# Split-precision matmuls in which the products with the low part of the weights come last

## The chip, the cores and the metric

One core of one Trainium2 chip runs the whole program in one launch. The metric is device time in microseconds (us). The core's engines are called by short names: PE is TensorE (PEld its weight loads), DVE is VectorE, ACT is ScalarE, POOL is GpSimd, SP is SyncE, which issues the transfers of the weights. SBUF is the core's working memory, PSUM the small memory into which PE accumulates.

## The reference

256 tokens of width 1024 in float32 go through two blocks. The first has a mixer of two attention kinds and then a feed-forward layer (PEER) that picks 128 of 16384 experts for each token. The second has two layers, each a mixer, a convolutional gated feed-forward and a gated input. Around each part stands a root-mean-square norm. Cut to what matters here:

```python
def peer_ffn(xn, w_query, subkeys, u_tab, v_tab):
    q = (xt @ w_query).reshape(T, 8, 2, 128)
    s = einsum('thpd,hpkd->thpk', q, subkeys)          # scores of 2 x 128 sub-keys
    ...                                                # top 16 per half, top 16 of 256 sums
    act = gelu(einsum('thkd,td->thk', u_tab[expert], xc))
    w = gate * act
    return einsum('thk,thkd->td', w, v_tab[expert])

def second_block(...):
    for i in range(2):
        hn = rmsnorm(h, mix_norm[i])
        h = h + (mixer_ab(hn, ...) if i == 0 else mixer_c(hn, ...))
        h = h + conv_glu_ffn(rmsnorm(h, ffn_norm[i]), ...)
        gate = sigmoid(rmsnorm(h, ple_norm[i]) @ ple_gate[i])
        h = h + gate * (p[i] @ ple_proj[i])
```

## The kernel before

**Split products.** PE multiplies in a rounded 32-bit type. To keep float32 accuracy, each operand is split in two: a high part, which is the value rounded, and a low part, the rest. A product is then three matmuls into one PSUM bank: high by high, high by low, low by high. Activations are split once per norm into xTh and xTl (L301 to L303: ACT copies the high part, DVE subtracts). Weights are split as they stream in: `wstart` (L104) has SP load tiles of 128 x 1024 into the ring `raw`, `wsplit` (L111) has ACT copy the high part `hi` (L114) and then DVE or POOL subtract to get `lo` (L117). Which of the two takes a tile is set by a repeating pattern: "V" is DVE and "G" is POOL. Most stages have "V"; the stage with the top-k has "G", and the stage with the routing products, below, has "VG", which gives every other tile to POOL. The rings hold 3 raw, 4 hi and 4 lo tiles, and a few more where memory is free.

**The three loops that use them.** `xs` (L182) makes outputs with tokens on partitions: each half tile of weights takes 6 matmuls of 512 columns for each of the two token tiles. `ws` (L255) makes outputs with features on partitions: each half tile takes 24 matmuls of 256 columns, three for each of 8 slices k. `peer_v` (L933) sums over the experts' second table into four PSUM banks that stay open for the whole stage; each expert group takes 12 matmuls of 512 columns. In `peer_v` the first operand is split as well, into wh and wl, once for each group.

**Stages.** The program is a chain: first norm, mixer, query, top-k (beside `peer_u` for experts of the first half), routing products, `peer_v`, then the second block with `mixer_ab`, feed-forward, gate, block C, feed-forward and gate. At each seam, the last `xs` of a stage holds back some tiles so that the norm (`norm_tile`, L324) of token tile 0 is made while tile 1 is still multiplied. The norm is a sum of squares on ACT, nx on DVE (L339), a power on POOL (L340), xn on DVE (L346, three pieces), transposes on PE (`tsplit`, L359, matmuls at L362), and the split of the result. In this stretch DVE also makes `lo` for the next stage's first tiles. "The query" and "block C's keys" are the first `xs` calls behind two of these norms.

**The stage with the routing products.** Here two things run merged: `peer_u` (L876) for the experts of the second half, which is a `ws` and keeps PE busy, and `peer_g` (L898), which builds the gate of each token and expert. `peer_g` goes through 32 blocks of eight tokens, numbered from 0 here. In a block DVE makes two tiles E (L911, comparisons of the picked indices with an iota), then, twice, for four tokens each: ACT copies the one E to a float32 operand h (L916), DVE multiplies the other by the gate into another h (L917), PE makes four products of them in PSUM (`sm`, L921), and the result is multiplied on DVE into the table act (L927, act0 for the first half of the experts, act1 for as many of the second half as are already made) or copied by ACT where the activation isn't made yet (L929). `peer_u` applies the gelu on ACT (L886, L889) and multiplies by what is there (L887). So in each block DVE and ACT each have a dozen instructions from `peer_g`, `peer_u` and `wsplit`, whose shares change from block to block: act1 grows on DVE and shrinks on ACT.

**What sets the order.** Engines run their own queues in order. The order in each queue isn't written by hand: a scheduler, which has the program order, a cost for each instruction and the dependencies, places instructions on each engine; only a few are pinned to program order. So the order on DVE, ACT and POOL follows from when the scheduler finds operands to be ready and wanted, also where the code of these engines isn't touched.

## Time and profile before

| | us |
|---|---|
| median of 3 runs | 1646.69 |
| lowest, highest | 1646.3, 1653.85 |
| the profiled execution, its own time | 1641.96 |
| its span on the core | 1640.2 |
| PE busy | 1607.5 (98%) |
| DVE busy | 1206.6 (74%) |
| ACT busy | 943.2 (58%) |
| POOL busy | 290.2 (18%) |
| `lo` on DVE (L117) | 506.0, 413 instructions |
| `lo` on POOL (L117) | 249.2, 96 instructions |
| `hi` on ACT (L114) | 537.8, 509 instructions |

The profile is of one execution; its clock is the full one (0.999 granted). The busy shares are means over all stages. A matmul's busy time is counted with its modelled end, and matmuls overlap: rows that follow each other at a start-to-start distance of 0.11 us (256 columns) show a duration of 0.28 us. So lengths of PE's work are read from starts, not from durations. The same holds, by less, for DVE, whose instructions begin about 0.08 us before the one before has ended.

### The profile page before, as it was taken

To read this page: it belongs to the slowest core of one execution; us is meant where nothing else is said; L and a number is where in the kernel's file an instruction comes from. 1 tells how busy PE (TensorE), PEld (TensorE's weight loads), DVE (VectorE), ACT (ScalarE), POOL (GpSimd) and SP (SyncE) were. 2 spreads that over 40 slices of the span, in tenths; PEclk is the share of its full clock that TensorE was granted. 3 is DMA by queue.
4 is the path that set the end of the run, shared out by engine and by line. 5 is a ranking of instruction groups with operands and counts; after the bars stand their busy time and mean duration, and the time that the engine had idled before them with its cause. 6 is when DMAs were issued, how large, how long until landed. Compare 5 with 4: busy or idle time off the path is not lost.

```text
span 1640.2 us, 27505 instructions
## 1 busy us (share of the span) xinstructions
PE 1607.5 (98%) x10596; PEld 1435.0 (87%) x10596; DVE 1206.6 (74%) x2172; ACT 943.2 (58%) x1435; POOL 290.2 (18%) x145
## 2 busy tenths in 40 slices
PE   7999999999999999999999999989999999999998
PEld 5878999999999997888888879869998777899986
DVE  7766597908999996666555567878896686699845
ACT  5555545446666665555555557457664456576633
POOL 2000499993333220000000001100000000000000
PEclk9999999999999999999999999999999999999999
DMA  7536556554444446656666555437666662376661
GB/s 248 178 123 214 157 169 195 167 178 132 147 135 143 141 151 209 192 192 226 218 192 190 192 178 176 124 98 228 190 195 191 191 227 85 98 227 194 194 192 63
DMA packets 83200, 284.54 MB, mean 173 GB/s; under 512 B 10556, under 2 KB 14589, under 8 KB 82942
## 3 DMA queue, kind: packets, MB, share of 16 engines
q1 hardware_dynamic: 82924, 282.72, 54.8%
q8 instruction: 83, 1.36, 0.3%
q14 instruction: 47, 0.39, 0.1%
q10 hardware_dynamic: 146, 0.07, 0.0%
HBM read 280.64 MB, written 2.12 MB: 172 GB/s over the span
## 4 chain that ended last, share of the span: by engine, by line
PE 80%; DVE 15%; ACT 2%; issue 1%; DMA 1%; POOL 1%; SPq 0%; DVEq 0%; ACTq 0%; POOLq 0%
PE mm L957 21%; PE mm L268 11%; PE mm L269 11%; PE mm L270 11%; PE mm L214 6%; PE mm L213 6%; PE mm L212 6%; DVE h L917 5%; DVE lo L117 3%; DVE E L911 2%; DVE act L927 1%; PE sm L921 1%; PE sm L605 1%; PE sm L362 1%; PE sm L577 1%
## 5 line engine op out<-in xcount | busy, mean ns | idle before, releaser
L114 ACT ACTIVATE hi<-raw 128x1024 fp32r<-128x1024 f32 x509 | 537.8, 1059 | 329.7 <-PE mm L269 143.4
L117 DVE TENSOR_TENSOR lo<-raw,hi 128x1024 fp32r<-128x1024 f32 x413 | 506.0, 1230 | 172.9 <-ACT hi L114 169.8
L268 PE MATMUL mm<-xTh,hi 128*128 128x256 f32 x1992 | 559.1, 281 | 0.2
L269 PE MATMUL mm<-xTl,hi 128*128 128x256 f32 x1992 | 552.7, 278 | 0.0
L270 PE MATMUL mm<-xTh,lo 128*128 128x256 f32 x1992 | 552.4, 277 | 0.0
L268 PEld LDWEIGHTS mm<-xTh,hi 128*128 128x128 f32 x1992 | 374.5, 188 | 1.5 <-ACT xTh L302 0.7
L270 PEld LDWEIGHTS mm<-xTh,lo 128*128 128x128 f32 x1992 | 375.1, 188 | 0.0
L269 PEld LDWEIGHTS mm<-xTl,hi 128*128 128x128 f32 x1992 | 374.5, 188 | 0.6 <-DVE xTl L303 0.3
L117 POOL TENSOR_TENSOR lo<-raw,hi 128x1024 fp32r<-128x1024 f32 x96 | 249.2, 2615 | 204.8 <-ACT hi L114 194.5
L340 POOL TENSOR_TENSOR ny<-nx,expo 128x1 f32<-128x1 f32 x14 | 13.0, 925 | 928.2 <-DVE nx L339 928.2
L917 DVE TENSOR_TENSOR h<-E,gate 128x512 f32<-128x512 bf16 x64 | 116.0, 1815 | 1.8 <-PE sm L921 1.8
L213 PE MATMUL mm<-lo,xTh 128*128 128x512 f32 x256 | 102.3, 400 | 5.9 <-DVE lo L117 3.6
L212 PE MATMUL mm<-hi,xTh 128*128 128x512 f32 x256 | 103.6, 405 | 3.0 <-ACT xTh L302 2.8
L214 PE MATMUL mm<-hi,xTl 128*128 128x512 f32 x256 | 101.5, 398 | 0.5 <-DVE xTl L303 0.3
L916 ACT ACTIVATE h<-E 128x512 f32<-128x512 bf16 x64 | 72.3, 1133 | 43.3 <-DVE E L911 39.9
L1379 DVE SCALAR_TENSOR_TENSOR fc<-mm,cw,fc 128x255 f32<-128x255 f32 (+1 forms) x176 | 84.3, 479 | 3.1
L957 PE MATMUL mm<-hi,xTh 128*128 128x512 f32 x256 | 80.1, 394 | 1.4 <-DVE act L887 1.0
L911 DVE TENSOR_TENSOR E<-sel,iota 128x1024 bf16<-128x1024 bf16 x64 | 48.5, 795 | 43.7 <-POOL iota L905 38.1
L957 PE MATMUL mm<-hi,wh 128*128 128x512 f32 x256 | 79.9, 393 | 0.0
L957 PE MATMUL mm<-hi,xTl 128*128 128x512 f32 x256 | 79.6, 391 | 0.0
L957 PE MATMUL mm<-hi,wl 128*128 128x512 f32 x256 | 79.3, 391 | 0.0
L957 PE MATMUL mm<-lo,xTh 128*128 128x512 f32 x256 | 79.3, 390 | 0.0
(304 smaller groups left out, 2359.6 us busy)
## 6 DMA issues: line engine op xcount, KB each, us to landing
raw<-in_peer_uT SPq DMA_DIRECT2D x128, 512.0 KB, 3.9
raw<-in_peer_v SPq DMA_DIRECT2D x128, 512.0 KB, 4.3
raw<-in_ffn_up_ws SPq DMA_DIRECT2D x88, 512.0 KB, 4.7
raw<-in_ffn_down_a SPq DMA_DIRECT2D x40, 512.0 KB, 4.5
raw<-in_w_in_xs SPq DMA_DIRECT2D x20, 512.0 KB, 4.7
raw<-in_ab_ws SPq DMA_DIRECT2D x16, 512.0 KB, 4.6
raw<-in_ple_gate_xs SPq DMA_DIRECT2D x16, 512.0 KB, 4.2
raw<-in_w_query_ws SPq DMA_DIRECT2D x12, 512.0 KB, 4.9
```

The lines of the kernel that those rows point to most:

```text
L114: nc.scalar.activation(hi, raw, AF.Copy)
L117: x = eng.tensor_tensor(lo, raw, f32(hi), op=ALU.subtract)
L212: nc.tensor.matmul(p, xh[:, k, t], hi[:, w], start=n == 1 and kk == 0, stop=False)
L213: nc.tensor.matmul(p, xh[:, k, t], lo[:, w], start=False, stop=False)
L214: nc.tensor.matmul(p, xl[:, k, t], hi[:, w], start=False, stop=n == total[c] and kk == 1)
L268: nc.tensor.matmul(o, hi[:, w], xh[:, k, :], start=k == 0, stop=False)
L269: nc.tensor.matmul(o, hi[:, w], xl[:, k, :], start=False, stop=False)
L270: nc.tensor.matmul(o, lo[:, w], xh[:, k, :], start=False, stop=k == 7)
L911: v.tensor_tensor(E[q], x[:, :, None, :].to_broadcast([P, T1, P, T2]), iota[:, None].to_broadcast([P, T1, P, T2]), op=ALU.is_equal)
L917: v.tensor_tensor(B.rearrange("p t j -> p j t"), E[1][:, i], gate[:, None, t0:t0 + T2].to_broadcast([P, P, T2]), op=ALU.mult)
L957: nc.tensor.matmul(self.acc[tt][c], st_[:, t], mv[:, c * 512:c * 512 + 512], start=first and j == js[0] and i == 0, stop=j == last and i == 2)
L1379: v.scalar_tensor_tensor(c[:, o + sft:o + S], p[:, o:o + S - sft], cw[:, wi, j:j + 1], c[:, o + sft:o + S], op0=ALU.mult, op1=ALU.add)
```

## The change

In each of the three loops the matmuls that use the low part of the weights are put behind those that use the high part. In `xs`, for a half tile and a token tile, the order was high-high, high-low(weights), low-high for the first slice and again for the second; it becomes high-high for both, low-high for both, and then the two with `lo`. In `ws`, for a half tile, the three matmuls of each of 8 slices become 16 with `hi`, and behind them 8 with `lo`. In `peer_v`, where the weights are the moving operand, the 8 matmuls with `hi` for both token tiles come first and then the 4 with `lo`. The number of matmuls, their shapes, the flags that open and close a sum and the other engines' code stay. The sums are the same in another order. Lines below the edits are shifted by at most one in the new file.

```diff
--- before.py
+++ after.py
@@ -205,13 +205,12 @@
                 acc[tt, c] = self.mm_ps()
             p = acc[tt, c]
             n = seen[tt, c] = seen.get((tt, c), 0) + 1
-            for kk in range(2):
-                k = kp * 2 + kk
-                w = slice(kk * 512, kk * 512 + 512)
-                t = slice(tt * P, tt * P + P)
-                nc.tensor.matmul(p, xh[:, k, t], hi[:, w], start=n == 1 and kk == 0, stop=False)
-                nc.tensor.matmul(p, xh[:, k, t], lo[:, w], start=False, stop=False)
-                nc.tensor.matmul(p, xl[:, k, t], hi[:, w], start=False, stop=n == total[c] and kk == 1)
+            t = slice(tt * P, tt * P + P)
+            for x, y in ((xh, hi), (xl, hi), (xh, lo)):
+                for kk in range(2):
+                    nc.tensor.matmul(p, x[:, kp * 2 + kk, t], y[:, kk * 512:kk * 512 + 512],
+                                     start=n == 1 and kk == 0 and x is xh and y is hi,
+                                     stop=n == total[c] and kk == 1 and y is lo)
             if n == total[c]:
                 epi(tt, c, p)
             self.tick()
@@ -267,7 +266,8 @@
                     w = slice(k * P, k * P + P)
                     nc.tensor.matmul(o, hi[:, w], xh[:, k, :], start=k == 0, stop=False)
                     nc.tensor.matmul(o, hi[:, w], xl[:, k, :], start=False, stop=False)
-                    nc.tensor.matmul(o, lo[:, w], xh[:, k, :], start=False, stop=k == 7)
+                for k in range(8):
+                    nc.tensor.matmul(o, lo[:, k * P:k * P + P], xh[:, k, :], start=False, stop=k == 7)
                 if f == len(halves) - 1:
                     epi(q, p)
                 self.tick()
@@ -950,12 +950,13 @@
                     self.split(wh, wl, self.act(j + jj))
                     loaded[j + jj] = halves + (wh, wl)
             hi, lo, wh, wl = loaded[j]
-            for tt in tts:
-                t = slice(tt * P, tt * P + P)
-                for i, (st_, mv) in enumerate(((wh, hi), (wh, lo), (wl, hi))):
-                    for c in range(2):
-                        nc.tensor.matmul(self.acc[tt][c], st_[:, t], mv[:, c * 512:c * 512 + 512],
-                                         start=first and j == js[0] and i == 0, stop=j == last and i == 2)
+            for parts in (((wh, hi), (wl, hi)), ((wh, lo),)):
+                for tt in tts:
+                    t = slice(tt * P, tt * P + P)
+                    for st_, mv in parts:
+                        for c in range(2):
+                            nc.tensor.matmul(self.acc[tt][c], st_[:, t], mv[:, c * 512:c * 512 + 512],
+                                             start=first and j == js[0] and st_ is wh and mv is hi, stop=j == last and mv is lo)
         if norm is not None:
             wb = self.norm_w(norm)
         for j in js[:len(js) - hold]:
```

The scheduler places the other engines' instructions anew. Three places show what moves.

On DVE, the block of the routing stage that starts with E_842 (lo_851 is the tile of weights that DVE splits in this block, act1 the second half of the table). Before:

```order
L911 TENSOR_TENSOR E_842_6120<-sel_1415,iota_4272 128x1024
L911 TENSOR_TENSOR E_843_6121<-sel_1415,iota_4272 128x1024
L927 TENSOR_TENSOR act0_1911<-sm_833_6038,act0_1911 128x64x4
L887 TENSOR_TENSOR act1_4268<-mm_823_5958,act1_4268 128x2x160
L917 TENSOR_TENSOR h_6_82<-E_843_6121,gate_1416 128x128x4
L927 TENSOR_TENSOR act1_4268<-sm_833_6038,act1_4268 128x40x4
L117 TENSOR_TENSOR lo_851_6144<-raw_847_6137,hi_850_6143 128x1024
L927 TENSOR_TENSOR act0_1911<-sm_841_6085,act0_1911 128x64x4
L927 TENSOR_TENSOR act1_4268<-sm_841_6085,act1_4268 128x40x4
L917 TENSOR_TENSOR h_6_82<-E_843_6121,gate_1416 128x128x4
```

After:

```order
L911 TENSOR_TENSOR E_842_6120<-sel_1415,iota_4272 128x1024
L911 TENSOR_TENSOR E_843_6121<-sel_1415,iota_4272 128x1024
L117 TENSOR_TENSOR lo_851_6144<-raw_847_6137,hi_850_6143 128x1024
L887 TENSOR_TENSOR act1_4268<-mm_823_5958,act1_4268 128x2x160
L927 TENSOR_TENSOR act0_1911<-sm_833_6038,act0_1911 128x64x4
L917 TENSOR_TENSOR h_6_82<-E_843_6121,gate_1416 128x128x4
L927 TENSOR_TENSOR act1_4268<-sm_833_6038,act1_4268 128x40x4
L927 TENSOR_TENSOR act0_1911<-sm_841_6085,act0_1911 128x64x4
L927 TENSOR_TENSOR act1_4268<-sm_841_6085,act1_4268 128x40x4
L917 TENSOR_TENSOR h_6_82<-E_843_6121,gate_1416 128x128x4
```

lo_851 moved from behind the first h and the first act1 to the place behind the two E; the first act0 and L887 changed places.

On ACT, the same block (hi_859 is the high part of the tile that POOL splits). Before:

```order
L916 ACTIVATE h_5_81<-E_842_6120 128x128x4
L889 ACTIVATE act1_4268<-mm_823_5958 128x2x96
L929 ACTIVATE act1_4268<-sm_833_6038 128x24x4
L114 ACTIVATE hi_859_6227<-raw_857_6223 128x1024
L916 ACTIVATE h_5_81<-E_842_6120 128x128x4
L929 ACTIVATE act1_4268<-sm_841_6085 128x24x4
```

After:

```order
L916 ACTIVATE h_5_81<-E_842_6120 128x128x4
L889 ACTIVATE act1_4268<-mm_823_5958 128x2x96
L114 ACTIVATE hi_859_6227<-raw_857_6223 128x1024
L929 ACTIVATE act1_4268<-sm_833_6038 128x24x4
L916 ACTIVATE h_5_81<-E_842_6120 128x128x4
L929 ACTIVATE act1_4268<-sm_841_6085 128x24x4
```

The copy hi_859 moved ahead of the L929 that writes act1. In a block near the stage's end, that of E_919 with hi_936, ACT has before:

```order
L916 ACTIVATE h_5_81<-E_919_6736 128x128x4
L889 ACTIVATE act1_4268<-mm_900_6574 128x2x40
L114 ACTIVATE hi_936_6843<-raw_934_6839 128x1024
L929 ACTIVATE act1_4268<-sm_910_6654 128x10x4
L916 ACTIVATE h_5_81<-E_919_6736 128x128x4
```

And after:

```order
L916 ACTIVATE h_5_81<-E_919_6736 128x128x4
L889 ACTIVATE act1_4268<-mm_900_6574 128x2x40
L929 ACTIVATE act1_4268<-sm_910_6654 128x10x4
L114 ACTIVATE hi_936_6843<-raw_934_6839 128x1024
L916 ACTIVATE h_5_81<-E_919_6736 128x128x4
```

There the same pair changed places the other way round.

On DVE, the seam to block C (pg and h_6_82 are the end of the gate before, nx and xn the norm of the second token tile, lo_1968 to lo_1999 tiles of the next weights). Before:

```order
L1424 TENSOR_TENSOR pg_1949_13508<-pg_1949_13508,pj_11165 128x512
L117 TENSOR_TENSOR lo_1968_13557<-raw_1964_13550,hi_1967_13556 128x1024
L1425 TENSOR_TENSOR h_6_82<-pg_1949_13508,h_6_82 128x512
L117 TENSOR_TENSOR lo_1973_13578<-raw_1970_13573,hi_1972_13577 128x1024
L339 SCALAR_TENSOR_TENSOR nx_1953_13517<-ss_1950_13512 128x1
L117 TENSOR_TENSOR lo_1975_13582<-raw_1971_13575,hi_1974_13581 128x1024
L346 SCALAR_TENSOR_TENSOR xn_1955_13521<-h_6_82,ny_1954_13518,nw_1922_13396 128x256
```

After:

```order
L117 TENSOR_TENSOR lo_1968_13557<-raw_1964_13550,hi_1967_13556 128x1024
L1425 TENSOR_TENSOR pg_1949_13508<-pg_1949_13508,pj_11165 128x512
L117 TENSOR_TENSOR lo_1973_13578<-raw_1970_13573,hi_1972_13577 128x1024
L1426 TENSOR_TENSOR h_6_82<-pg_1949_13508,h_6_82 128x512
L117 TENSOR_TENSOR lo_1975_13582<-raw_1971_13575,hi_1974_13581 128x1024
L339 SCALAR_TENSOR_TENSOR nx_1953_13517<-ss_1950_13512 128x1
L117 TENSOR_TENSOR lo_1999_13692<-raw_1996_13687,hi_1998_13691 128x1024
L346 SCALAR_TENSOR_TENSOR xn_1955_13521<-h_6_82,ny_1954_13518,nw_1922_13396 128x256
```

Before, three `lo` stand between the multiplication of pg and xn, one of them between nx and xn. After, lo_1968 stands ahead of pg (it stood behind), and lo_1999, which stood behind the norm, stands between nx and xn.

## Rows read from the trace of the kernel before

**Rows 1.** The page: busy time by engine, share of the span, number of instructions

```profile
PE 1607.5 (98%) x10596; PEld 1435.0 (87%) x10596; DVE 1206.6 (74%) x2172; ACT 943.2 (58%) x1435; POOL 290.2 (18%) x145
```

**Rows 2.** Waits of PE: us in total, times, longest us

```profile
PE sm L362 <- DVE xn L346: 5.4, 9, 1.8
PE mm L213 <- DVE lo L117: 3.6, 7, 0.9
```

**Rows 3.** Windows: us, PE, PEld, DVE, ACT, POOL busy (instructions), PEclk, DMA, GB/s

```profile
520.00:550.00 30.00, 29.50 (x252) 28.82 (x252) 30.00 (x40) 19.60 (x31) 9.62 (x4) 1.00 0.46 137
```

**Rows 4.** Timeline, PE: start, duration, engine, line, output<-inputs, count [idle before <-releaser]

```profile
373.81 1.05 PE L921 MATMUL sm<-h,h 128*128 128x128 f32 x8
...
377.44 1.05 PE L921 MATMUL sm<-h,h 128*128 128x128 f32 x8
...
608.86 1.05 PE L921 MATMUL sm<-h,h 128*128 128x128 f32 x8
```

**Rows 5.** Timeline, DVE, one block of the routing stage

```profile
525.17 1.26 DVE L911 TENSOR_TENSOR E<-sel,iota 128x1024 bf16<-128x1024 bf16 x2
526.35 0.41 DVE L927 TENSOR_TENSOR act<-sm,act 128x256 f32<-128x256 f32 x1
526.68 0.47 DVE L887 TENSOR_TENSOR act<-mm,act 128x320 f32<-128x320 f32 x1
527.08 1.08 DVE L917 TENSOR_TENSOR h<-E,gate 128x512 f32<-128x512 bf16 x1
528.01 0.31 DVE L927 TENSOR_TENSOR act<-sm,act 128x160 f32<-128x160 f32 x1
528.24 1.21 DVE L117 TENSOR_TENSOR lo<-raw,hi 128x1024 fp32r<-128x1024 f32 x1
529.37 0.64 DVE L927 TENSOR_TENSOR act<-sm,act 128x256 f32<-128x256 f32 x2
529.93 3.04 DVE L917 TENSOR_TENSOR h<-E,gate 128x512 f32<-128x512 bf16 x1
532.83 1.26 DVE L911 TENSOR_TENSOR E<-sel,iota 128x1024 bf16<-128x1024 bf16 x2
```

**Rows 6.** Timeline, ACT and POOL, the same block

```profile
527.19 0.33 ACT L889 ACTIVATE act<-mm 128x192 f32<-128x192 f32 x1
528.36 0.25 ACT L929 ACTIVATE act<-sm 128x96 f32<-128x96 f32 x1 [0.83 <-DVE act L927]
528.50 1.05 ACT L114 ACTIVATE hi<-raw 128x1024 fp32r<-128x1024 f32 x1
...
529.63 2.40 POOL L117 TENSOR_TENSOR lo<-raw,hi 128x1024 fp32r<-128x1024 f32 x1 [5.26 <-ACT hi L114]
```

**Rows 7.** Timeline, PE, the first weight tiles of the program

```profile
19.42 0.51 PE L213 MATMUL mm<-lo,xTh 128*128 128x512 f32 x1 [1.25 <-POOL lo L424]
...
30.49 0.50 PE L213 MATMUL mm<-lo,xTh 128*128 128x512 f32 x1 [0.70 <-DVE lo L117]
```

**Rows 8.** Timeline, PE, the first tiles of the query

```profile
147.99 0.50 PE L213 MATMUL mm<-lo,xTh 128*128 128x512 f32 x1 [0.63 <-DVE lo L117]
```

**Rows 9.** Timeline, PE and DVE, the first tiles of block C

```profile
1327.08 0.50 PE L213 MATMUL mm<-lo,xTh 128*128 128x512 f32 x1 [0.94 <-DVE lo L117]
...
1330.40 1.54 DVE L346 SCALAR_TENSOR_TENSOR xn<-h,ny,nw 128x256 f32<-128x256 f32 x3 [0.44 <-POOL ny L340]
```

**Rows 10.** Timeline, DVE, starts of blocks 8, 12, 23 and 31

```profile
425.95 1.97 DVE L911 TENSOR_TENSOR E<-sel,iota 128x1024 bf16<-128x1024 bf16 x1 [0.92 <-ACT h L916]
...
457.05 1.26 DVE L911 TENSOR_TENSOR E<-sel,iota 128x1024 bf16<-128x1024 bf16 x2
...
540.50 1.27 DVE L911 TENSOR_TENSOR E<-sel,iota 128x1024 bf16<-128x1024 bf16 x2
...
601.13 1.27 DVE L911 TENSOR_TENSOR E<-sel,iota 128x1024 bf16<-128x1024 bf16 x2
```

## The prediction

> **What bounds the kernel now.** I read the busy table first: TensorE (PE) is busy for 98% of the span, with as many weight loads as matmuls [rows 1]. The change neither adds nor removes a matmul, so it can only win or lose what PE spends waiting: 1640.2 less 1607.5 is 32.7 us, of which the view of waits gives a low part of the weights (lo) only a small share: 3.6 us in 7 waits on VectorE's (DVE) L117, beside 5.4 us on the normalised activations xn [rows 2]. Most waits stand at the seams between two stages, where the first weight tiles of the next stage are split by the same DVE that makes the norm. Then I looked for a stage in which PE isn't the bound. There is one: the stage with the routing products (peer_g, 367 to 609 us), where DVE is busy for 30.00 of 30 us while PE is at 29.50 [rows 3]. PE's own pace there shows early, before it waits: its groups of L921 start 3.63 us apart, two in a block of eight tokens, so 7.26 us a block [rows 4], less than the blocks take (below). So the stage ends when DVE ends, and what counts is the order in which DVE, ScalarE (ACT) and GpSimd (POOL) stand, which the change also moves.
>
> **A block of that stage, before.** From the block at 525.17 to the next at 532.83 are 7.66 us [rows 5]: two E (1.18 from start to start of what follows), act from PSUM 0.33, L887 0.40, h 0.93, act 0.23, lo 1.13, two act 0.56, h 2.90. The same h takes 1.08 us the first time and 3.04 the second. What differs is POOL's lo (2.40 us from 529.63, [rows 6]): the second h ends at 532.97, 0.94 us after POOL ends at 532.03. So h, which reads two SBUF operands, stands until POOL is through, and the four act, which read PSUM, don't (two of them run 0.64 us at 529.37 beside it). Without the stall the block is 7.66 - 1.96 = 5.70 us. The next block starts 0.80 us after POOL ends, which makes block length = POOL's start in the block + 3.20. POOL starts 1.13 us after ACT's L114, and that one starts 0.14 after ACT's L929, which waits for the first act1 of DVE: 528.32, 528.36, 528.50, 529.63.
>
> The Trainium skill's page "SBUF — State Buffer" (the list under its diagram) says that VectorE and GpSimd share a port pair as an exclusive lock: whoever starts first holds it for the whole instruction, and a VectorE instruction with two SBUF inputs blocks fully. The trace agrees, with 3.04 against 1.08 us. By that rule alone, with nothing of POOL's 2.40 us over PSUM reads, a block would be 5.70 + 2.40 = 8.10 us and the sum below would be that of the third rival.
>
> **The change, part by part.**
> *Matmuls of xs, ws and peer_v.* Their number and shapes stay, each keeps its own weight load [rows 1]: 0 us. A lo is wanted after 4 of 6 matmuls instead of after 1 (xs), after 16 of 24 instead of after 2 (ws): it can't be wanted earlier. In ws and peer_v it hides nothing that shows, since no wait for lo stands there [rows 2]. In peer_v wl is wanted two matmuls sooner; I cost that at 0, since no wait on wl shows, between 0 and +1 us at the stage's first tile.
> *Start.* PE waits 1.25 us at 19.42 and 0.70 at 30.49 for lo [rows 7]. In the new order four matmuls stand before each pair with lo, so at most both waits go, -1.95. But the fourth lo and the second norm tile come from DVE at the same time as before, and PE, which gets to them sooner, waits for the latter: at worst 0. I take -0.8, under the middle, since the later of the two waits is that for a lo that comes last.
> *Seam to the query.* PE waits 0.63 us for lo at 147.99 [rows 8]. DVE now splits lo_294 before the norm's xn, where it stood behind it, so xn comes about one lo (1.13 us [rows 5]) later. PE needs xn only after all 24 matmuls instead of after 19; it then waits for xTl where it waited for lo, less long: -0.5 us, between -0.63 and +0.5 (one lo less the 0.63).
> *Seam to block C's keys.* The wait of 0.94 at 1327.08 goes [rows 9]. But DVE has one more lo (1.13) in front of xn, which was ready at 1330.40 and on which the next transposes depend: PE now waits there for about 1.7 us: +0.6 us net.
> *Other seams and the attention parts*, where the order moves by up to 18 matmuls: 0, between -1 and +1 us in all, from the sizes of the three above.
> *The routing stage, 32 blocks.* lo moves from behind the first h to directly behind the two E, on DVE; on ACT the L114 for POOL's tile stands before L929 in blocks 11 to 22 and behind it in 23 to 31 (before: behind in 2 to 24, ahead in 25 to 31).
> - Blocks 2 to 7: same chain with the same members, 0.
> - Blocks 8 to 11 (425.95 to 457.05 are 31.10 us, [rows 10]): here POOL still falls on E, which then takes 1.97 us and waits for ACT's h. Before, block 8 left that state in one long block: with three of about 7.5, it was 31.10 - 22.5 = 8.6. After, that block comes three later, behind three that stay in the state at about 7.7 each, so 23.1 and 8.7: 31.8, +0.7 us.
> - Blocks 12 to 22 (457.05 to 540.50 are 83.45 us for 11, so 7.59 each): L887 ends at 1.18 + 1.13 + 0.47 = 2.78, L889 starts 0.04 later and takes 0.33, L114 overlaps it by 0.1 and starts at 3.05; POOL 4.18; block 7.38. 11 x 0.21 = -2.3 us. PE's 7.26 is no bound yet.
> - Blocks 23 to 30 (540.50 to 601.13 are 60.63 us for 8, so 7.58 each): L929 is first again and waits for the first act1, which now stands behind lo: it ends at 2.31 + 0.40 + 0.33 + 0.31 = 3.35, L114 at 3.53, POOL 4.66, block 7.86. L887 and act1 grow with the block: from 160 to 256 columns act goes from 0.31 to 0.41 [rows 5], so with 144 more columns in L887 and 72 in act1 at the end of the stretch it is 0.15 + 0.07 more, 8.08. Mean 7.97: 8 x 0.39 = +3.1 us.
> - Block 31: the last h's come about 2 us later in it and PE's slack there covers all but +0.6 us.
> Sum of the stage +2.1 us; bounds: -6.2 us (63 groups of L921 from 373.81 at PE's pace of 3.633 would end 6.2 us before the 608.86 at which the stage's last group starts [rows 4]) and +9.7 us (19 blocks at 8.10 instead of 7.59).
>
> Total: -0.8 - 0.5 + 0.6 + 2.1 = +1.4 us. The profiled execution was 1641.96 us (span 1640.2), so 1643.4 on its scale; the three runs' median is 1646.69, 4.7 us above it, and on that scale I forecast **1648 us**: no change that can be measured (within 0.5%, 8.2 us, about what a measurement of this kernel can tell).
>
> **The rivals.**
> 1. *Cover wins.* The hi products hide every wait for lo and POOL's stall moves onto PSUM reads, so that PE sets the routing stage: -6.2 there and, of the 3.6 us of waits for lo and the 1.25 at the start, 4.9, those at the seams to the norms come back: about -3 is left: -9 us, 1637.5. For it: blocks 12 to 22 do come near PE's pace. Against it: in blocks 23 to 31 the order on ACT goes the other way, and at the seams DVE is the next that is late.
> 2. *The change does nothing*, because waits for lo only trade place with waits for xn and h: within 2 us of 1646.7. For it: 30 of the 32.7 us without work aren't waits for lo. It lies inside the forecast's own range.
> 3. *POOL's lock takes the block.* If POOL's lo lands on E or h from its first to its last ns in blocks 12 to 30, a block is 8.10 us: 19 x 0.51 = +9.7, with the seams +9, 1656. It decides from the point where ACT's L114 starts later than 3.7 us into a block, or where the state of blocks 2 to 10 (E stalled) doesn't end at block 11. For it: DVE has no idle time to give [rows 3]. Against it: in blocks 12 to 22 L114 no longer waits for act1.
> 4. *Late norms.* At each seam DVE puts one lo more before xn: 7 seams by 1.1 us, +8 with no gain from lo, 1655. Against it: only two of the seams have that order.
>
> **How the numbers follow.** Forecast and rival 2 together 0.70, rival 1 0.13, rivals 3 and 4 0.17. The forecast's own range is 1643 to 1652. To leave out no more than 2 in 10 the range takes in most of rivals 1, 3 and 4: 1638 to 1657. Faster by over 0.5% (below 1638.5) 0.13, within 0.70, slower (above 1654.9) 0.17.
>
> **What would show it.** In the profile after: the waits of PE on L117 fall from 3.6 us to under 1, those on xn rise above 5.4. In the routing stage a block of 7.4 us near 500 us with one h of about 2.7 us, and of about 8.0 near 580 us with an h over 3 us; POOL's lo 4.2 and then 4.7 to 4.9 us into the block. The last L921 group starts 2 us later than 608.86. It is wrong if the late blocks stay at 7.5 or below (then POOL's start doesn't follow act1), if blocks 12 to 22 stay above 7.6, or if a seam moves by more than 2 us.

## The result

| | us |
|---|---|
| before, median of 6 runs beside the changed kernel | 1646.51 (1640.29 to 1656.83) |
| after, median of 6 runs | 1667.56 (1665.53 to 1669.21) |
| ratio | 1.0123, 95% interval 1.01 to 1.0146 |
| span of the profiled execution, before and after | 1640.2 and 1664.7 |

The kernel became slower by 1.2%, 21 us in the medians and 24.5 us between the two profiles. The forecast was 1648 us and no change. The busy line of the page after, to set against [rows 1]:

```profile
PE 1625.7 (98%) x10596; PEld 1453.8 (87%) x10596; DVE 1198.8 (72%) x2172; ACT 932.9 (56%) x1435; POOL 290.6 (17%) x145
```

PE is busy 18.2 us longer with the same 10596 matmuls. More work isn't there, so PE waits more (span less busy time is 39.0 instead of 32.7 us, 6 of the 24.5) and the same matmuls run slower (the other 18). No term of the forecast allowed for the second. The table takes the start of the same matmul in both traces, all through the program, and notes where the difference grows:

| stretch | the difference grows by, us |
|---|---|
| up to the first matmul with weights | -0.8 |
| from there to the query's seam | -0.6 |
| the query's seam | -0.4 |
| routing stage, to its last L921 | +2.8 |
| its seam to peer_v, until the difference stands still | +3.5 |
| rest of peer_v, mixer_ab | +0.5 |
| first feed-forward layer, with the wait ahead of it | +6.1 |
| gate, first half of block C (to its first L605) | +1.8 |
| attention of block C (first to last L605) | +5.6 |
| rest of block C | 0.0 |
| second feed-forward layer, with the wait ahead of it | +6.1 |

**The routing stage** went as forecast. A block of the middle stretch on DVE, as [rows 5]:

```profile
499.93 1.28 DVE L911 TENSOR_TENSOR E<-sel,iota 128x1024 bf16<-128x1024 bf16 x2
501.13 1.22 DVE L117 TENSOR_TENSOR lo<-raw,hi 128x1024 fp32r<-128x1024 f32 x1
502.26 0.43 DVE L887 TENSOR_TENSOR act<-mm,act 128x272 f32<-128x272 f32 x1
502.61 0.41 DVE L927 TENSOR_TENSOR act<-sm,act 128x256 f32<-128x256 f32 x1
502.94 1.10 DVE L917 TENSOR_TENSOR h<-E,gate 128x512 f32<-128x512 bf16 x1
503.88 0.83 DVE L927 TENSOR_TENSOR act<-sm,act 128x136 f32<-128x136 f32 x3
504.62 2.85 DVE L917 TENSOR_TENSOR h<-E,gate 128x512 f32<-128x512 bf16 x1
507.30 1.28 DVE L911 TENSOR_TENSOR E<-sel,iota 128x1024 bf16<-128x1024 bf16 x2
```

507.30 less 499.93 is 7.37 us (forecast 7.38), and the second h takes 2.85 us. In a late block ACT waits for the first act1 again before L114, and POOL starts 4.87 us into the block that begins at 577.11 and ends 8.06 us later (forecast 7.97):

```profile
577.11 1.27 DVE L911 TENSOR_TENSOR E<-sel,iota 128x1024 bf16<-128x1024 bf16 x2
...
582.17 3.16 DVE L917 TENSOR_TENSOR h<-E,gate 128x512 f32<-128x512 bf16 x1
585.17 1.27 DVE L911 TENSOR_TENSOR E<-sel,iota 128x1024 bf16<-128x1024 bf16 x2
```
```profile
580.75 0.20 ACT L929 ACTIVATE act<-sm 128x40 f32<-128x40 f32 x1 [0.45 <-DVE act L927]
580.86 1.05 ACT L114 ACTIVATE hi<-raw 128x1024 fp32r<-128x1024 f32 x1
```
```profile
581.98 2.40 POOL L117 TENSOR_TENSOR lo<-raw,hi 128x1024 fp32r<-128x1024 f32 x1 [5.67 <-ACT hi L114]
```

First and last group of PE there, as [rows 4]; 237.8 us lie between them, 235.05 before the change:

```profile
371.99 1.05 PE L921 MATMUL sm<-h,h 128*128 128x128 f32 x8
...
609.80 1.05 PE L921 MATMUL sm<-h,h 128*128 128x128 f32 x8
```

**The seam to peer_v** did not go as forecast. The waits of PE, as [rows 2] (columns: us in all, times, longest):

```profile
PE sm L362 <- DVE xn L346: 6.3, 11, 1.5
PE sm L921 <- DVE h L917: 3.9, 8, 0.6
...
PE mm L958 <- ACT xTh L302: 2.9, 1, 2.9
...
PE mm L211 <- DVE lo L117: 2.3, 2, 1.7
```

The 2.9 us stand in front of peer_v, where before it was 0.39. On ACT and on DVE, before:

```profile
612.52 0.16 ACT L929 ACTIVATE act<-sm 128x8 f32<-128x8 f32 x1
612.58 0.71 ACT L302 ACTIVATE xTh<-act 128x256 fp32r<-128x256 f32 x2
```
```profile
611.68 1.07 DVE L927 TENSOR_TENSOR act<-sm,act 128x248 f32<-128x248 f32 x3 [0.25 <-ACT act L889]
612.67 1.21 DVE L117 TENSOR_TENSOR lo<-raw,hi 128x1024 fp32r<-128x1024 f32 x1
```

And after:

```profile
611.82 0.18 ACT L929 ACTIVATE act<-sm 128x8 f32<-128x8 f32 x1 [0.54 <-DVE sink L1281]
611.93 1.06 ACT L114 ACTIVATE hi<-raw 128x1024 fp32r<-128x1024 f32 x1
615.00 0.18 ACT L929 ACTIVATE act<-sm 128x8 f32<-128x8 f32 x1 [2.01 <-DVE act L927]
615.11 1.06 ACT L114 ACTIVATE hi<-raw 128x1024 fp32r<-128x1024 f32 x1
616.07 0.40 ACT L302 ACTIVATE xTh<-act 128x256 fp32r<-128x256 f32 x1
```
```profile
613.02 1.23 DVE L117 TENSOR_TENSOR lo<-raw,hi 128x1024 fp32r<-128x1024 f32 x1 [1.21 <-ACT hi L114]
614.17 0.74 DVE L927 TENSOR_TENSOR act<-sm,act 128x256 f32<-128x256 f32 x2
```

Read it as a ring: the lo that now stands ahead of act on DVE waits for ACT's hi, act waits behind it, ACT's L929 waits for act, and the first operand of peer_v (L302) stands behind that and one more hi. Before, act stood ahead of lo, and L302 followed L929 at once.

This wait is 2.5 of the 3.5 us. The other 1.0 us grows behind it, where PE's granted clock is at half, 1.2 GHz, from 618.8 to 622.2 us (0.85 and 0.72 in the means of the two windows); before, it was 1.00 there. The columns are those of [rows 3]:

```profile
616.00:620.00 4.00, 2.80 (x9) 1.92 (x10) 3.80 (x9) 3.13 (x10) 0.00 (x0) 0.85 0.76 283
620.00:624.00 4.00, 4.00 (x15) 3.18 (x13) 2.27 (x5) 1.51 (x3) 0.00 (x0) 0.72 0.06 25
```

**The feed-forward layers: the same matmuls at another pace.** Fifty us from the middle of the second layer, before and then after; PE is busy all the time, its clock is 1.00, and the first number in brackets is how many matmuls ran in it:

```profile
1450.00:1500.00 50.00, 50.00 (x443) 50.00 (x443) 45.66 (x75) 34.05 (x55) 0.00 (x0) 1.00 0.66 197
```
```profile
1500.00:1550.00 50.00, 50.00 (x427) 50.00 (x426) 43.80 (x73) 32.33 (x53) 0.00 (x0) 1.00 0.59 185
```

Worked out from the starts themselves, two matmuls of 256 columns are 113.3 ns apart before and 117.8 after; with 512 columns it is 228.9 and 233.3. Below these are called the quick and the slow pace. In none of the 16 profiles does the pace change inside an unbroken stream of one shape, its first twenty matmuls aside: where it changes, a wait, smaller matmuls or another shape stand in between. The slow pace isn't a matter of the changed kernel alone: the kernel before, in which nothing is reordered, has it from 277 to 365 us:

```profile
200.00:250.00 50.00, 50.00 (x444) 50.00 (x443) 49.93 (x141) 24.66 (x30) 48.05 (x17) 1.00 0.55 168
...
300.00:350.00 50.00, 50.00 (x427) 50.00 (x426) 26.80 (x16) 26.22 (x30) 49.15 (x18) 1.00 0.58 179
```

A layer is 1056 matmuls of 256 columns and 251 of 512 in one run: 1056 x 4.5 + 251 x 4.4 ns = 5.9 us by this sum; from its first matmul to its end each layer measured 5.6 us more. The remaining 0.5 of the 6.1 is the wait ahead of it. What stands ahead of the first layer also changed. ACT and PE before, then after:

```profile
1114.30 0.60 ACT L1407 ACTIVATE pj<-mm 128x512 f32<-128x512 f32 x1 [0.69 <-PE mm L214]
1114.80 1.15 ACT L302 ACTIVATE xTh<-sm 128x256 fp32r<-128x256 f32 x3
```
```profile
1114.10 1.03 PE L362 MATMUL sm<-ident,xn 128*128 128x128 f32 x8
1115.22 0.50 PE L268 MATMUL mm<-xTh,hi 128*128 128x256 f32 x2
```
```profile
1118.85 1.06 ACT L114 ACTIVATE hi<-raw 128x1024 fp32r<-128x1024 f32 x1 [0.31 <-PE mm L211]
1119.81 0.58 ACT L1408 ACTIVATE pj<-mm 128x512 f32<-128x512 f32 x1
1120.29 1.14 ACT L302 ACTIVATE xTh<-sm 128x256 fp32r<-128x256 f32 x3
```
```profile
1119.11 1.04 PE L362 MATMUL sm<-ident,xn 128*128 128x128 f32 x8
1120.72 0.51 PE L267 MATMUL mm<-xTh,hi 128*128 128x256 f32 x2 [0.58 <-ACT xTh L302]
```

After, a copy hi stands ahead of the last pj and the norm's xTh, and PE starts the layer 1.61 us behind the first transpose instead of 1.12: 0.85 instead of 0.36 us behind the last one.

**The attention of block C: the clock.** The same 28 matmuls of L605, before and then after, with the window after:

```profile
1377.03 3.24 PE L605 MATMUL sm<-cv,aPT 128*128 128x64 f32 x28
```
```profile
1390.71 6.07 PE L605 MATMUL sm<-cv,aPT 128*128 128x64 f32 x28
```
```profile
1386.00:1400.00 14.00, 13.71 (x64) 12.72 (x63) 5.37 (x21) 6.38 (x19) 0.00 (x0) 0.53 0.18 57
```

The granted clock is 0.53 of full speed in these 14 us, so nearly all of them at 1.2 GHz. Ahead of the fall PE had waited 1.67 us for ACT's apr. The kernel before had such a wait too (1.73 us, in front of 1372) and kept 1.00 in that one execution; the experiments show that in other executions it does not.

The Trainium skill ("TensorE: Matmul & The Clock Gate", section "What's actually happening") says that a block which watches how busy PE has been passes all or half of the clock's pulses; the trace agrees: 0.50 from 1388 to 1400 us, 1.00 ahead of the fall and behind it.

### The profile page after: what moved, and what is told of

It reads as the page before. It is cut to its first block, busy times and chain, and to the rows that moved or that the text cites. A ratio compares the mean times of both kernels' runs of the same rounds, so it can differ in the third digit from the quotient of the medians.

```text
span 1664.7 us, 27438 instructions
## 1 busy us (share of the span) xinstructions
PE 1625.7 (98%) x10596; PEld 1453.8 (87%) x10596; DVE 1198.8 (72%) x2172; ACT 932.9 (56%) x1435; POOL 290.6 (17%) x145
## 4 chain that ended last, share of the span: by engine, by line
PE 78%; DVE 16%; issue 3%; ACT 2%; POOL 1%; DMA 0%; POOLq 0%; SPq 0%; DVEq 0%; ACTq 0%
PE mm L958 21%; PE mm L211 18%; PE mm L267 11%; PE mm L270 11%; PE mm L268 11%; DVE h L917 5%; DVE lo L117 4%; DVE E L911 1%; DVE act L927 1%; PE sm L605 1%; PE sm L362 1%; PE sm L577 1%; DVE xn L346 1%; DVE act L887 1%; PE sm L1188 1%
## 5 line engine op out<-in xcount | busy, mean ns | idle before, releaser
L114 ACT ACTIVATE hi<-raw 128x1024 fp32r<-128x1024 f32 x509 | 537.2, 1058 | 494.2 <-PE mm L958 167.0
L117 DVE TENSOR_TENSOR lo<-raw,hi 128x1024 fp32r<-128x1024 f32 x413 | 507.2, 1233 | 257.9 <-ACT hi L114 256.5
L267 PE MATMUL mm<-xTh,hi 128*128 128x256 f32 x1992 | 481.6, 283 | 1.2 <-ACT xTh L302 1.2
L268 PE MATMUL mm<-xTl,hi 128*128 128x256 f32 x1992 | 474.5, 279 | 0.0
L117 POOL TENSOR_TENSOR lo<-raw,hi 128x1024 fp32r<-128x1024 f32 x96 | 250.2, 2624 | 204.2 <-ACT hi L114 193.8
L270 PE MATMUL mm<-xTh,lo 128*128 128x256 f32 x1992 | 272.6, 279 | 0.0
L270 PEld LDWEIGHTS mm<-xTh,lo 128*128 128x128 f32 x1992 | 249.4, 189 | 0.1
L917 DVE TENSOR_TENSOR h<-E,gate 128x512 f32<-128x512 bf16 x64 | 109.2, 1709 | 0.0
L916 ACT ACTIVATE h<-E 128x512 f32<-128x512 bf16 x64 | 72.4, 1135 | 39.6 <-DVE E L911 32.7
L911 DVE TENSOR_TENSOR E<-sel,iota 128x1024 bf16<-128x1024 bf16 x64 | 53.2, 868 | 45.8 <-POOL iota L905 38.2
L211 PE MATMUL mm<-hi,xTh 128*128 128x512 f32 x256 | 82.9, 404 | 2.4 <-ACT xTh L302 2.2
L211 PE MATMUL mm<-lo,xTh 128*128 128x512 f32 x256 | 81.1, 398 | 4.1 <-DVE lo L117 2.3
L958 PE MATMUL mm<-hi,xTh 128*128 128x512 f32 x256 | 79.7, 393 | 3.6 <-ACT xTh L302 2.9
L211 PE MATMUL mm<-hi,xTl 128*128 128x512 f32 x256 | 81.9, 399 | 1.1 <-DVE xTl L303 1.1
L958 PE MATMUL mm<-hi,xTl 128*128 128x512 f32 x256 | 80.0, 395 | 0.0
L921 PE MATMUL sm<-h,h 128*128 128x128 f32 x512 | 68.3, 276 | 4.1 <-DVE h L917 3.9
```

What stands on the lines that cost most here:

```text
L114: nc.scalar.activation(hi, raw, AF.Copy)
L117: x = eng.tensor_tensor(lo, raw, f32(hi), op=ALU.subtract)
L211: nc.tensor.matmul(p, x[:, kp * 2 + kk, t], y[:, kk * 512:kk * 512 + 512], start=n == 1 and kk == 0 and x is xh and y is hi, stop=n == tot ...
L267: nc.tensor.matmul(o, hi[:, w], xh[:, k, :], start=k == 0, stop=False)
L268: nc.tensor.matmul(o, hi[:, w], xl[:, k, :], start=False, stop=False)
L270: nc.tensor.matmul(o, lo[:, k * P:k * P + P], xh[:, k, :], start=False, stop=k == 7)
```

## Experiments

There were two theories at the start. The first: the slower pace and the lower clock are states of PE that depend on how it comes into a stretch, and the change only alters the odds. The second: the new order itself makes the matmuls of ws slower. Each run's ratio is to runs of the kernel before beside it, with the 95% interval; it isn't exactly the quotient of the two medians. The kernel before itself had medians between 1645.6 and 1651.4 us in these series, so medians of different series compare to a few us only. The pace of a layer is read as above (443 or 444 matmuls in 50 us, or 426 or 427). The code cuts leave out what stands around them.

### The kernel before once more, and each loop alone

No edit in `again`; in the others one of the three pieces of the diff (ws, xs or peer_v).

> The kernel before, unchanged, for a second profile. In the first profile PE's split products of 256 columns start either 113.3 or 117.8 ns apart for whole stretches (117.8 from 277 to 365 us and in the query of mixer_ab, 113.3 in both feed-forward layers). Theory 'pace is a state': the pace of each stretch is set where PE restarts in front of it, so it may come out otherwise in another execution of the same program; a feed-forward layer at the slow pace costs 1056 x 4.5 ns = 4.8 us and its down part 251 x 4.4 ns = 1.1 us, so 1640.2 plus 0, 5.9 or 11.7 us. Rival 'pace is fixed by the program': the same stretches are slow as before, span 1640 within 1 us.

1646.42 us, 1.0006 (0.998 to 1.0032); profiled span 1643.9. Both layers ran at the quick pace again, but the first run of ws in mixer_ab (982 to 1011 us in the first profile), slow there (117.8), was quick (113.3), and the clock fell in block C:

```profile
1370.00:1390.00 20.00, 19.37 (x90) 16.95 (x91) 10.43 (x50) 9.50 (x31) 0.00 (x0) 0.66 0.12 40
```

So one program has both paces at one place, and the kernel before has the fall as well; in this profile the attention of block C takes 5.6 us longer by it, as much as in the changed kernel. Of 31 executions in this series (21 beside the others and these 10) 10 had a mean clock of 0.999 or 1.0, the rest 0.991 to 0.996; spans were 1638.4 to 1639.5 at 0.999 and mostly 1643.6 to 1646.1 below, so a fall costs some 5 us. Two runs at 1.0 took 1643.3 and 1644.0, about a slow layer more, but they have no profile. The first profile was one of the lucky ones. Neither theory of the expectation holds in full: the pace ahead of the routing stage came out alike, that of mixer_ab did not.

> Only the loop ws puts the products with lo last. Theory 'the new order of ws is what makes the feed-forward slow': both layers at 117.8 ns, +11.7 us there; routing stage +2.6 and the seam to peer_v +3.3 us, which come from where the scheduler puts lo on DVE; attention of block C as before: span about 1640 + 17.6 = 1658. Rival 'pace is a state': the routing stage and the seam give the same 5.9 us, and the feed-forward layers 0, 5.9 or 11.7.

1653.80 us, 1.006 (1.0029 to 1.0091). The pace of both layers is quick:

```profile
1500.00:1550.00 50.00, 50.00 (x444) 50.00 (x443) 45.47 (x74) 34.86 (x57) 0.00 (x0) 1.00 0.66 193
```

The new order of ws is in that stretch, and its matmuls are no slower: the second theory falls. In this profile the routing stage costs 2.9 us and its seam 1.1, not 3.3: PE waits 2.76 us in front of peer_v, but the clock doesn't fall there. The clock also fell in block C, for another 5.6 us, where the expectation had no change.

> Only the loop xs puts the products with lo last. Theory 'the new order of ws is what makes the feed-forward slow': feed-forward at 113.3 ns, routing stage as before (blocks 7.6 us), the attention of block C with the fall of the clock to half as in the kernel with all three, +6.5 us: span about 1640 - 1.8 + 6.5 + 1 = 1646. Rival 'pace is a state': the same, plus 0, 5.9 or 11.7 us from the feed-forward layers.

1659.58 us, 1.0097 (1.0061 to 1.0132): more than either theory had without slow layers. The second layer was slow (427 matmuls), without a change in ws; the first was quick. The clock fell in block C, as both theories had it, and also at 80 to 90 us (0.53), where PE lost about 4.5 us.

> Only the loop peer_v puts the products with lo last. Theory 'the new order of ws is what makes the feed-forward slow': no stage but peer_v differs; the seam to it between 0 and +3.3 us, span 1640 to 1644. Rival 'pace is a state': 0, 5.9 or 11.7 us more from the feed-forward layers, although nothing there is changed.

1646.73 us, 1.0006 (0.9982 to 1.0029). peer_v alone changes nothing that can be measured, and the seam's wait was 0.5 us. In its profile the clock fell at 80 to 90 us (0.58) and not in block C, so the place isn't fixed either.

### Can a stop turn the pace?

Here three transposes are put into each layer's ws (in after_t4 it is `range(4)`):

```diff
+                if f == 1:
+                    d = self.sm_ps()
+                    for i in range(3):
+                        self.tc.keep_in_program_order(nc.tensor.transpose(d[:, i * P:(i + 1) * P], self.ident, self.ident))
                 if f == 10:
                     for x in extra:
```

> The changed kernel with three more transposes (128 x 128, of the identity, into a PSUM bank that nobody reads) between the second and the third pair of tiles of each feed-forward's ws, 0.33 us of extra work each. In six profiles so far a group of three transposes in the top-k stage turned PE's pace from 113.3 to 117.8 ns a matmul, and groups of 4, 8 and 32 did not. Theory 'the pace is a state with two values that an odd group of small matmuls turns over': in each layer the pace behind the three is the other one than ahead of them; if it is 117.8 ahead as in the profile of the changed kernel, the rest runs at 113.3, 960 x 4.5 + 251 x 4.4 ns = 5.4 us less a layer: 1667.6 - 10.8 + 0.7 = 1657.5 us. Rival 'the new order of ws makes the matmuls slower': 117.8 on both sides, 1668. Rival 'any stop of the stream draws the pace anew': either pace, without regard to what was ahead.

> The same with four such transposes. Theory 'a state that an odd group turns over': the pace behind the four is the one ahead of them, 1667.6 + 0.9 = 1668.5 us if it is 117.8 ahead. Rival 'any stop of the stream draws the pace anew': either pace; rival 'order of ws': 117.8 and 1668.5.

after_t3: 1657.79 us, 1.0062 (1.0041 to 1.0083); after_t4: 1661.09, 1.0072 (1.005 to 1.0094). Windows of after_t3 (PE's share; the three transposes stand at 1133.96 and 1450.28):

```profile
1124.00:1133.00 9.00, 9.00 (x78) 9.00 (x78) 8.90 (x10) 5.16 (x6) 0.00 (x0) 1.00 0.73 218
1140.00:1180.00 40.00, 40.00 (x356) 40.00 (x355) 36.64 (x59) 27.44 (x45) 0.00 (x0) 1.00 0.66 195
1440.00:1450.00 10.00, 10.00 (x87) 10.00 (x86) 9.80 (x12) 5.84 (x8) 0.00 (x0) 1.00 0.70 222
1460.00:1500.00 40.00, 40.00 (x342) 40.00 (x341) 35.18 (x57) 25.65 (x43) 0.00 (x0) 1.00 0.62 190
```

40 us with 356 matmuls are quick, with 342 slow. In the first layer the transposes turned slow into quick, in the second they changed nothing, and in the one profile of each, four did exactly the same as three. PE doesn't wait at them, so it is not a stop but the smaller matmuls in between. Work was added, and the kernel is 6 to 10 us quicker by the medians; from after to after_t3 the first layer is 5.0 us shorter, and in after_t3's profile the clock didn't fall in the attention of block C, which is another 5.6. So the pace isn't a property of the order alone. My theory of an odd group fell.

> The kernel before with a fourth transpose (a repeat of the third) in both groups of three of the top-k stage. Theory 'a state that an odd group turns over': the 744 matmuls behind the first group stay at 113.3 instead of 117.8 ns, 3.3 us, less 0.2 for the two transposes: routing stage starts 3.1 us earlier, 1646 - 3.1 = 1643 us. Rival 'that stretch is slow for what runs beside it (POOL 98% busy, transfers)': 117.8 as in all six profiles, 1646.2 us.

1647.44 us, 1.0011 (0.9993 to 1.0029): four transposes also ended in the slow pace, which buries the odd group once more. In after_t4's profile the 264 and 600 matmuls ahead of that place ran slow and the 744 behind it quick, the reverse of all the others; so the stretch isn't slow for what runs beside it either.

### The routing stage and its seam

```diff
+                    if self.u_pattern == "VG" and self.lo_pattern == "VG":
+                        nc.tensor.matmul(o, lo[:, w], xh[:, k, :], start=False, stop=k == 7)
```

(and the separate loop over lo only elsewhere.)

> The changed kernel with the old order of ws in the stage with the routing products alone. Theory 'the routing stage and the seam behind it lose to where lo stands on DVE and ACT': blocks 23 to 30 back from 8.06 to 7.58 us and 12 to 22 from 7.37 to 7.59, the stage 2.6 us shorter, and PE's wait of 2.9 us at the seam to peer_v gone (0.4): 5.5 us less than the changed kernel, 1662 us if the feed-forward layers and the attention of block C are as slow as in it. Rival 'the seam's wait comes from the new order of peer_v': the 2.9 us stay, 2.6 us less.

1653.04 us, 1.0042 (1.0014 to 1.007). The last L921 starts 1.4 us earlier than before instead of 0.9 later, no wait on xTh shows at the seam, the clock doesn't fall there, and peer_v's first matmul with wl (its tile is named xTl there) starts 1.6 us earlier instead of 4.2 later: 5.8 us, with the new order of peer_v in place. So the order of ws in this stage is needed for the seam's loss, and the rival, peer_v's order by itself, falls. `ws_only` lost only 1.1 us there, so part of the 3.5 us comes from the orders together; how they share it, and the fall of the clock in it, isn't shown. The rest of the gain is a first layer at the quick pace in that profile.

### What makes the slow pace likely

In pj_old; in pj_new the condition is reversed (`is not`), in the kernel before:

```diff
-            for x, y in ((xh, hi), (xl, hi), (xh, lo)):
...
+            if xT is getattr(self, "pT", None):
+                parts = [(kk, x, y) for kk in range(2) for x, y in ((xh, hi), (xh, lo), (xl, hi))]
+            else:
+                parts = [(kk, x, y) for x, y in ((xh, hi), (xl, hi), (xh, lo)) for kk in range(2)]
...
```

> The changed kernel with the old order of xs in one small product alone, that of the gated input (pT, 24 of 768 or so steps), which stands right ahead of each feed-forward. On ACT the copy hi then stands behind the norm's xTh again, as before the change. Theory 'the slow pace is caught where PE restarts behind the longer wait for xTh (0.85 instead of 0.36 us)': the wait is 0.36 us again, both layers start at 113.3 ns as in all ten streams with 0.36 us so far (8 of 10 with 0.85 were slow): 1667.6 - 2 x 0.5 - 11.7 = 1655 us. Rival 'the pace is slow for the new order of the whole program, wherever': at least one layer stays at 117.8 ns, 1661 us or more.

1663.42 us, 1.0076 (1.0049 to 1.0103). In the profiled execution, span 1656.2, both layers begin behind 0.36 us and are quick, as expected; but three of the five runs had spans of 1661.6 to 1664.3, and what they lost has no profile. This confirms the expectation by half.

> The kernel before with the new order of xs in one small product alone, that of the gated input (24 matmuls of 512 columns for each layer, twice 24 of about 9100 split products), which turns ACT's copy hi and the norm's xTh around ahead of each feed-forward. Theory 'the longer wait for xTh ahead of the feed-forward (0.85 us) is what makes the slow pace likely' (10 of 12 streams that began behind 0.85 us were slow, 1 of 18 behind 0.36): wait 0.85 at both, each layer slow with a chance of about 0.8, so 1 + 0.8 x 11.7 = 10 us over the kernel before, 1656 us. Rival 'these 48 matmuls are too few to matter, the pace goes with the order as a whole': 1646 us, 113.3 ns in both layers.

1656.03 us, 1.007 (1.0041 to 1.01). PE ahead of the first layer:

```profile
1116.92 1.03 PE L363 MATMUL sm<-ident,xn 128*128 128x128 f32 x8
1118.53 0.62 PE L269 MATMUL mm<-xTh,hi 128*128 128x256 f32 x3 [0.58 <-ACT xTh L303]
```
```profile
1500.00:1550.00 50.00, 50.00 (x427) 50.00 (x426) 43.80 (x72) 32.71 (x54) 0.00 (x0) 1.00 0.61 185
```

48 reordered matmuls of some 9100 give half of the loss: 1.61 us from the first transpose to the layer, and both layers slow, each 5.6 us longer. (The clock also fell at 81 us in this profile, where PE lost some 4.5 us, so part of the difference between the medians may be that.) Over all 16 profiles: behind 0.85 us 12 of 14 starts were slow (7 profiles), behind 0.36 us 1 of 18 (9 profiles). Two things limit this. All starts behind 0.85 us also have the new order in the product right ahead, so whether the wait or that order makes the slow pace likely isn't separated. And the runs without a profile, three of pj_old above all, hint that the pace is slow behind 0.36 us more often than 1 in 18.

### The clock in block C

The attribute `warm` is set around block C's first attention alone; in warm8 the 4 is an 8:

```diff
+                for i in range(4 if getattr(self, "warm", 0) and tt else 0):
+                    nc.tensor.transpose(pt[:, i % 4 * P:i % 4 * P + P], self.ident, self.ident)
```

> The kernel before with 16 more transposes of the identity (4 ahead of each group of the second token tile) in the attention of block C, in places where PE waits: 16 x 0.11 = 1.8 us of work, of which the waits of 1.7 and 0.8 us cover up to 1.5. In 2 of 3 executions of the kernel before the granted clock is 0.994 to 0.996, in the others 0.999; the profile of the second execution has 0.61 and 0.71 there from 1370 to 1390 us. Theory 'PE's clock falls to half there for what PE does in the stretch ahead, and this costs 5.5 us': the clock stays at 1.00 and runs lie at 1640 to 1641 us with the other states as they are, median 1641 instead of 1646. Rival 'the fall comes from the load of the whole chip or from chance': the same share of runs at 0.995, median 1647.

> The same with 32 transposes (8 ahead of each group), 3.5 us of work, of which up to 2.5 is covered. Theory: the clock stays at 1.00, median 1642. Rival: 1648.

warm4: 1641.39 us, 0.9961 (0.9944 to 0.9979); warm8: 1644.76, 0.996 (0.9939 to 0.9981). The window of warm4 against that of `again`:

```profile
1370.00:1390.00 20.00, 19.08 (x130) 16.27 (x130) 13.49 (x64) 12.87 (x43) 0.00 (x0) 1.00 0.15 43
```

130 matmuls instead of 90, 12 of them added ones, at a clock of 1.00 instead of 0.66. In 8 of 10 runs of warm4 the clock was 0.998 or 0.999, and in all 6 of warm8 0.999 or 1.0; beside them 14 of 16 runs of the kernel before (median 1647.58) were at 0.991 to 0.996. So the fall hangs on what PE does there and isn't chance alone. The kernel before with these transposes beats both kernels.

### Put together

> The changed kernel with the three places put right that the runs so far point to: the old order of ws in the routing stage (5.6 us: stage 2.6, seam to peer_v 3), the old order of xs in the product of the gated input (PE's wait of 0.85 us ahead of the feed-forward, and with it the slow pace, up to 11.7), and 16 transposes that hold the clock in the attention of block C (5.5). The new order stays everywhere else: all other xs and ws, and peer_v. Theory 'the order of the products costs nothing by itself': 1667.6 - 5.6 - 11.7 - 6.5 = 1643.8, within 4 us of the kernel before with the same transposes (1641.4). Rival 'the new order costs something of its own elsewhere': over 1650.

1649.67 us, 1.0011 (0.9974 to 1.0048), beside runs of the kernel before with a median of 1651.41, in a series in which that kernel was slower than in the others. Three places put right take the whole loss away as far as this can tell; but warm4 was 0.996, so up to some 8 us may still belong to the new order elsewhere. The profile (span 1645.0, 5.9 us above that of warm4) still shows the clock down at 1060 to 1070 (0.85) and at 1370 to 1380 us (0.88); against warm4 it loses 3.4 us in mixer_ab and 3.4 in block C, where these falls lie. The measured time is between the two expectations, and the question stays open.

> The changed kernel with the 16 transposes in the attention of block C alone. Theory 'in the changed kernel the clock falls there in every run and costs 6.5 us': clock up from 0.991-0.994 to 0.997 or more, 1667.6 - 6.5 + 0.3 = 1661.4 us. Rival 'the stretch is longer for the order of the products, not for the clock': 1667 us.

1659.04 us, 1.0043 (1.0013 to 1.0073): 8 us less than the changed kernel by the medians of two series, 6.2 expected. The mean clock rose to 0.993 to 0.996 only. In the profile the long fall in the attention is gone but for 3.4 us at 1390, and falls of 3.4 us stay at 619, 1073 and 1346 us.

## Why the prediction was wrong

Point by point, by its own steps, between the two profiles:

- *Start*, -0.8: measured -0.6 from the first matmul with weights on. The wait of 0.70 for the second lo went; the 1.25 us at 19.42 stayed (1.25 at 18.19). The other -0.8 of the table lies ahead of the first matmul with weights, which starts anywhere from 10.25 to 11.61 us in the 16 profiles, in either order, so it isn't the change's.
- *Seam to the query*, -0.5: -0.4. *Seam to block C's keys*, +0.6: +0.7; PE waits 1.49 us for xn there, forecast 1.7.
- *Routing stage*, +2.1: +2.8. Blocks 12 to 22 give -2.4 (forecast -2.3), blocks 23 to 30 +3.8 (forecast +3.1), since they take 8.06 us from the first of them on and not 7.97 in the mean. That POOL's start follows act1 and the block follows POOL's end, held. In these late blocks rival 3 came true by its own sign: ACT's L114 starts 3.75 us into the block, and 8.06 is nearly its 8.10. In blocks 12 to 22 it did not. Rival 1 failed, since PE waits for h in the late blocks; but "PE's 7.26 is no bound yet" holds only at the quick pace. From 478 to 545 us of the changed kernel PE runs without a wait at the slow pace, 3.72 us a group of L921, 7.44 a block, which is more than DVE's 7.37. The late blocks, in which PE waits again, hide that.
- *Block 31*, "PE's slack there covers all but +0.6 us": the last L921 comes 0.8 us later by this block, so its number held, but the lateness doesn't end there. Behind the stage it is another +3.5: 2.5 for the ring of hi, lo, act and L929 on two engines and 1.0 where the clock is at half. I counted DVE's lateness and not that ACT's first operand of peer_v is queued behind an instruction that waits for DVE. The rows show the ring; wsr shows that the loss goes with the order of ws in this stage.
- *Other seams and the attention parts*, "0, between -1 and +1 us": wrong by more than all the rest. The turn on ACT ahead of each feed-forward costs only 0.5 us by itself, but PE comes out of that seam at the slow pace, and each layer then takes 5.6 us more. pj_new shows that the order of the small product ahead is enough for it. The attention of block C took 5.6 us more in this profile because the clock fell there.
- *"Their number and shapes stay, each keeps its own weight load: 0 us"*: this is the step that failed in its thinking. It takes a matmul's price as fixed by its shape, and so does the sentence that opens the prediction, that the change "can only win or lose what PE spends waiting". The trace of before showed two prices for one shape (444 and 427 matmuls in 50 us), and I had not looked. In the two layers this term is 11.2 us.
- *The total on the median's scale.* I took the 4.7 us between profile and median as noise to add. They were, in most runs, a fall of the clock. After the change the mean clock was 0.991 to 0.994 in all six runs; of the 31 runs of the kernel before counted under `again`, 21 were at 0.991 to 0.996. So the medians differ by less than the two profiles: 21 us, not 24.5. With the 5.6 us of block C's fall on both sides some 19 us are left, an estimate.
- *What would show it.* The waits on lo (L117) fell from 3.6 to 2.3 us and not under 1: two new ones, 0.62 and 1.66 us, stand at 975 and 980 us, at the seam to mixer_ab. The waits on xn rose to 6.3, as forecast. The last L921 came 0.9 us later instead of 2. And one seam moved by more than 2 us, which the prediction itself names as a sign of being wrong.

The named steps (start, two seams, routing stage) sum to +2.5 us against +1.4 forecast; the 23 us that the forecast lacks lie in places that it had put at 0. Rival 4, slower by 8 us, had the right sign and the wrong cause: the waits on xn grew by 0.9 us in all.

What stays open: whether the longer wait or the order of the product ahead makes the slow pace likely, and why; why the same transposes turned it in one layer and not in the other; and what makes the clock fall at one place in some executions and not in others.

## What to carry to other kernels

Before costing a reordering at nothing, count the matmuls in equal windows of the trace: if the same shape shows two paces, the way PE enters a long stretch can be worth more than the waits that the change is about. Follow a moved split through all engines that share its ring (hi on ACT, lo on DVE, what stands behind each), above all in the last steps ahead of a long stretch. And compare several runs' spans and clocks with the profiled one before taking it as typical: sixteen idle transposes in the place where the clock falls gained 0.4%, and none of the three reordered loops alone made the kernel faster.

## What the runs showed of the hardware that was not expected

- Streams of matmuls with a weight load each have two paces at full clock: 113.3 and 117.8 ns for 256 columns, 228.9 and 233.3 ns for 512. Once a stream has one, it holds over a thousand matmuls (1056 in a layer). The Trainium skill ("TensorE: Matmul & The Clock Gate", section "Wait — 56ns, not 53.3ns?") has one value for matmuls back to back at full clock, the columns at 2.4 GHz and about 2.5 ns more; an estimate from it is 109.2 and 215.8. Neither measured pace is that, and here the measurement decides.
- At 1.2 GHz the 28 small matmuls took 6.07 instead of 3.24 us; 16 more transposes of 0.11 us in the waits ahead kept the clock up in most runs and made the kernel 0.4% quicker.
